# Feed-forward of a two-block kernel in four parts of 3, 3, 3 and 2 pieces instead of three of 4, 4 and 3, with a seventh pair of tiles for split weights

## The chip, the cores and the metric

The kernel runs on one core of one Trainium2 chip. The metric is the device time of one execution in microseconds. The kernel before took 1610.94 us (median of three runs, 1607.69 to 1611.66). The program is written in Python; a scheduler turns it into one fixed instruction list per engine, and the engines then run their lists in order and wait for each other through semaphores. Engines are named as in the profile: PE (TensorE matmul), PEld (its weight load), DVE (VectorE), ACT (ScalarE), POOL (GpSimd), SP (the queue that issues the weight loads).

## The reference, cut to what matters

Two transformer-like blocks run one after the other on 256 tokens of width 2048, all in float32. The change lies in the feed-forward of the first block:

```python
D_MODEL, SEQ, D_FF = 2048, 256, 5632
h2 = _rmsnorm(x, ffn_norm_w[l])
g, u = jnp.split(jnp.einsum('bsd,df->bsf', h2, w_gate_up[l]), 2, axis=-1)
x = x + jnp.einsum('bsf,fd->bsd', jax.nn.silu(g) * u, w_down[l])
```

Ahead of it stand the first block's mixer and its output projection, behind it a norm and the whole second block (input projection, short convolution, two kinds of attention, output projection), which the change does not touch.

## The kernel before, in words

**Split operands.** Every large product is made three times with operands cut into a high and a low part. A weight tile `raw` of 256 rows by 512 columns (512 KB) is loaded by SP; ACT writes its high part `wh` (L63), DVE the low part `wl` = raw - wh (L54), and PE multiplies high by high, high by low, and low by high. `parts_of` (L120) does the two splits and takes the pair of tiles (`wh`, `wl`) from a pool. In the feed-forward the list `more_w` (L642) says which pool is next: it is turned round by one at each split and holds `wsp` (four pairs) and `wsx` (two pairs), six pairs in all. A pair comes free when the last matmul that reads it is done, so PE sets when ACT and DVE may split the next weights; DVE in turn, by finishing a split, sets when a raw tile (eight of them) comes free for SP's next load.

**Units.** The left operands, already split, lie in units: tiles of 128 x 4 x 2 x 256 from `upool`, which has eight. During the feed-forward four units hold the normed input (`x1u`), and the others take the hidden activations.

**Pieces and parts.** The 5632 hidden columns are cut into eleven pieces of 512. `hidden_pre(f, between)` (L651) makes one piece: eight steps over 256 input rows each. Five steps split a gate and an up tile and make 24 matmuls; three steps (2, 4 and 6) use a seven-product form with sums of weights (`Ta`, `Tb`) and split tiles of 1024, 1024, 1024 and 512 columns for 21 matmuls. A piece thus has 183 matmuls of 512 columns, 22 splits, and at its end a chain of ten additions on DVE, two silu on ACT and two products (`hd`, L51) on DVE. It uses all eight PSUM banks.

**The turn.** The piece's result `hd` has tokens on partitions and must be turned round: `turn` (L735) makes eight 128 x 128 transposes on PE in two groups of four, and after each group ACT and DVE read the bank and write half a unit. The second group goes into the same bank as the first, so it waits for the first group to be read. Inside a part the turn of one piece is made in the middle of the next one, after its step 5 (`between(X4)`, L684), in the bank of that piece's accumulator X4, whose last six matmuls (step 8) then go into it again, once the second group has been read. The last piece of a part is turned by itself after it (`waiting(bank(...))`, L757).

**Down projection.** At the end of a part, `proj` (L149) multiplies the part's units with `w_down`, four times over, for 512 output columns each: 24 matmuls and two weight tiles for each unit and column group. `residual` (L593) then adds the two PSUM banks to `X` on DVE. In the last part each column group is also normed by its weight, transposed and split into `x2u`, for the second block.

**What sets the order.** The scheduler places ready instructions by priority; loads, splits and the end of a piece are raised by 4000 places. It may mix the matmuls of down projection and of the next or last piece on PE, as long as their operands come in order.

Of the kernel before, what the change touches and what calls it, by code (L numbers as in the profile page):

```python
# [9 lines left out]
F32R = mybir.dt.float32r  # L10
# [19 lines left out]
def tile_two_blocks(  # L30
# [12 lines left out]
    wsp = ctx.enter_context(tc.tile_pool(name="wsp", bufs=4))  # L43
    upool = ctx.enter_context(tc.tile_pool(name="upool", bufs=8))
# [8 lines left out]
    def tt(out, a, b, op):  # L53
        nc.vector.tensor_tensor(out=out, in0=a, in1=b, op=op)  # L54
# [7 lines left out]
    def act(out, in_, func=AF.Copy, **kw):  # L62
        nc.scalar.activation(out=out, in_=in_, func=func, **kw)  # L63
# [4 lines left out]
    def bank(shape):  # L68
        return phd.tile(shape, F32, tag="h", name="h")
# [5 lines left out]
    def new_unit():  # L75
        return upool.tile([128, 4, 2, T], F32R, tag="u", name="u")
# [10 lines left out]
    def unit_from(src, scale, u=None, js=range(2), keep=None):  # L87
        u = u or new_unit()
        for j in js:
            ps = transposed(src, j)  # L90
            if keep is not None:
                keep(j, ps)
            for a in range(2):
                k = 2 * j + a
                act(u[:, k, 0], ps[:, a], scale=scale(k))
                stt(u[:, k, 1], ps[:, a], scale(k), u[:, k, 0].bitcast(F32), ALU.mult, ALU.subtract)
        return u
# [8 lines left out]
    more_w = []  # L106
# [13 lines left out]
    def parts_of(raw, pool=None):  # L120
        if pool is None:
            pool = more_w[0] if more_w else wsp
            if more_w:
                more_w.append(more_w.pop(0))
        wh = pool.tile(list(raw.shape), F32R, tag="wh", name="wh")
        wl = pool.tile(list(raw.shape), F32R, tag="wl", name="wl")
        act(wh, raw)
        tt(wl, raw, wh.bitcast(F32), ALU.subtract)
        return wh, wl

    def split(w, r0, nk, c0, n, pool=None):
        with tc.high_priority(4000):
            return parts_of(load(w, r0, nk, c0, n), pool)
# [15 lines left out]
    def proj(units, w, c0, first_nk=2, after=None):  # L149

        pt = [mm_bank() for t in range(NT)]
        last = len(units) - 1
        for i, (u, r0) in enumerate(units):
            grow = u if callable(u) else None
            nk = first_nk if i == 0 else 2
            for k0 in range(0, 4, nk):
                if grow is not None and k0 % 2 == 0:
                    u = grow(k0 // 2)
                wh, wl = split(w, r0 + k0 * 128, nk, c0, CW)
                for a in range(nk):  # L160
                    k = k0 + a
                    mh, ml = in_turn(wh[:, a]), in_turn(wl[:, a])
                    for t in range(NT):
                        sl = slice(t * 128, (t + 1) * 128)
                        st, sp = i == 0 and k == 0, i == last and k == 3
                        nc.tensor.matmul(pt[t], lhsT=u[:, k, 0, sl], rhs=mh, start=st, stop=False)  # L166
                        nc.tensor.matmul(pt[t], lhsT=u[:, k, 0, sl], rhs=ml, start=False, stop=False)  # L167
                        nc.tensor.matmul(pt[t], lhsT=u[:, k, 1, sl], rhs=mh, start=False, stop=sp)  # L168
            if after is not None:
                after(i)  # L170
        return pt
# [37 lines left out]
    def stats_piece(st, src, c):  # L209
        for t in range(NT):  # L210
            nc.vector.bn_stats(out=st[:, t, c], in_=src(t))
# [341 lines left out]
    for hf in range(2):  # L553
# [5 lines left out]
        for j in range(2):  # L559
# [4 lines left out]
            for a in range(2):  # L564
                k = 2 * j + a
# [7 lines left out]
        u = new_unit()  # L573
# [8 lines left out]
    def xc(c):  # L582
        return lambda t: X[:, t, c * CW:(c + 1) * CW]

    def xk(c):
        return lambda t, k: X[:, t, c * CW + k * 128:c * CW + (k + 1) * 128]
# [6 lines left out]
    def residual(pt, c):  # L593
        for t in range(NT):
            x_c = two(xc(c)(t))
            tt(x_c, ordered(pt[t]), x_c, ALU.add)
# [42 lines left out]

    more_raw.extend([wraw, ff.enter_context(tc.tile_pool(name="wraw2", bufs=4))])  # L640
    wsx = ff.enter_context(tc.tile_pool(name="wsx", bufs=2))
    more_w.extend([wsp, wsp, wsx, wsp, wsp, wsx])  # L642

    def tri(pt, left, right, st, sp):
        (xh, xl), (wh, wl) = left, right
# [5 lines left out]
    def hidden_pre(f, between):  # L651
# [14 lines left out]
        for p in range(8):  # L666
# [21 lines left out]
            with tc.high_priority(4000):  # L688
                g_ = load(w_gate_up, r0, 2, f * CW, CW)
                u_ = load(w_gate_up, r0, 2, DFF + f * CW, CW)  # L690
                B1 = parts_of(g_)
                Ta, Tb = (fp.tile([128, 2, CW], F32, tag=n, name=n) for n in ("Ta", "Tb"))
                tt(Ta[:, 0], u_[:, 0], g_[:, 0], ALU.subtract)
                tt(Ta[:, 1], u_[:, 1], u_[:, 0], ALU.subtract)
                W13 = parts_of(Ta)
                tt(Tb[:, 0], u_[:, 1], Ta[:, 0], ALU.subtract)
                tt(Tb[:, 1], g_[:, 1], Tb[:, 0], ALU.subtract)
                W24 = parts_of(Tb)
                B22 = parts_of(u_[:, 1:2])
# [35 lines left out]
    def turn(h, u):  # L735
        def run(ps):
            ps = ps.rearrange("p (a t) -> p a t", a=2)
            for j in range(2):
                for a in range(2):
                    for t in range(NT):  # L740
                        nc.tensor.transpose(
                            out=ps[:, a, t * 128:(t + 1) * 128],
                            in_=h[:, t, 256 * a + j:256 * (a + 1):2], identity=ident,
                        )
                unit_split(u, ps, 2 * j, 2)
        return run

    st = new_stats()
    x2u = []
    for part in (range(0, 4), range(4, 8), range(8, 11)):  # L750
        gu = []
        waiting = lambda ps: None
        for f in part:
            h = hidden_pre(f, waiting)
            gu.append((new_unit(), f * CW))
            waiting = turn(h, gu[-1][0])
        waiting(bank([128, CW]))  # L757
        for c in range(4):
            residual(proj(gu, w_down, c * CW), c)
            if part[-1] == 10:  # L760
                x2u.append(unit_from(xk(c), lambda k, c=c: wfg[:, 4 * c + k:4 * c + k + 1]))
                stats_piece(st, xc(c), c)
# [291 lines left out]
    for u, r0 in out_units:  # L1054
        for k0 in (0, 2):
            pool = lw if len(parts) < 6 else wsp
            parts.append((u, k0, split(w_out2, r0 + k0 * 128, 2, 3 * CW, CW, pool)))
    for t in range(NT):
        sl = slice(t * 128, (t + 1) * 128)
        n = CW if t == 0 else CW // 2  # L1060
        for c0 in range(0, CW, n):
            pt = mm_bank()[:, :n]
            cs = slice(c0, c0 + n)
            for i, (u, k0, (wh, wl)) in enumerate(parts):
                for a in range(2):
                    k = k0 + a
# [7 lines left out]
            part = small.tile([128, 1], F32, tag="part", name="part")  # L1074
# [50 lines left out]
```

## Time and profile before

| | before |
|---|---|
| median of three runs | 1610.94 us |
| the profiled execution's own time | 1610.98 us |
| its span, first to last instruction | 1609.2 us |
| PE, DVE, ACT busy, share of the span | 99%, 77%, 55% |
| granted TensorE clock, mean | 0.999 |
| the feed-forward in the trace | about 530 to 1205 us |

The profiled execution took 1.8 us more than its span. In the views a row has a start and a duration in microseconds, the engine, the line, and the tiles as out<-in; in square brackets stands the idle time of the engine ahead of it and what ended it. Matmuls overlap: a 512-column matmul is shown with 0.38 us, but the next one starts 0.216 us after it.

### The profile page before, as it was taken

To read this page: it belongs to the slowest core of one execution; us is meant where nothing else is said; L and a number is where in the kernel's file an instruction comes from. 1 tells how busy PE (TensorE), PEld (TensorE's weight loads), DVE (VectorE), ACT (ScalarE), POOL (GpSimd) and SP (SyncE) were. 2 spreads that over 40 slices of the span, in tenths; PEclk is the share of its full clock that TensorE was granted. 3 is DMA by queue.
4 is the path that set the end of the run, shared out by engine and by line. 5 is a ranking of instruction groups with operands and counts; after the bars stand their busy time and mean duration, and the time that the engine had idled before them with its cause. 6 is when DMAs were issued, how large, how long until landed. Compare 5 with 4: busy or idle time off the path is not lost.

```text
span 1609.2 us, 22431 instructions
## 1 busy us (share of the span) xinstructions
PE 1591.8 (99%) x8433; PEld 1415.7 (88%) x8433; DVE 1241.6 (77%) x1726; ACT 886.0 (55%) x1156; POOL 23.0 (1%) x61
## 2 busy tenths in 40 slices
PE   9999999999999999999999999999999999999997
PEld 7999999999988888888888888888889889998987
DVE  7769768765667899976699975799777999766754
ACT  4657557544555665543565554456546545555644
POOL 2000000000000000000000000000000000000000
PEclk9999999999999999999999999999999999999999
DMA  8765466466686666676666676566756567556564
GB/s 283 225 192 166 145 178 188 143 186 209 203 301 216 183 199 207 203 236 202 191 208 199 188 241 205 181 210 198 242 151 207 146 199 222 182 157 199 163 218 140
DMA packets 164604, 318.36 MB, mean 198 GB/s; under 512 B 10184, under 2 KB 10848, under 8 KB 164496
## 3 DMA queue, kind: packets, MB, share of 16 engines
q1 hardware_dynamic: 162240, 312.25, 62.3%
q10 hardware_dynamic: 1760, 4.47, 0.8%
q8 instruction: 66, 1.08, 0.3%
q0 software_dynamic: 496, 0.21, 0.1%
q14 instruction: 42, 0.34, 0.1%
HBM read 313.74 MB, written 3.15 MB: 197 GB/s over the span
## 4 chain that ended last, share of the span: by engine, by line
PE 82%; DVE 12%; issue 3%; DMA 2%; ACT 0%; DVEq 0%; POOLq 0%; ACTq 0%; POOL 0%
PE p L194 18%; PE p L168 11%; PE p L167 11%; PE p L166 11%; PE p L195 9%; DVE wl L54 6%; PE p L648 3%; PE p L649 3%; PE p L647 3%; PE h L448 2%; PE h L649 2%; PE h L648 2%; PE h L647 2%; DMA raw<-in_w_gate_up_dram 2%; PE p L192 1%
## 5 line engine op out<-in xcount | busy, mean ns | idle before, releaser
L54 DVE TENSOR_TENSOR wl<-raw,wh 128x1024 fp32r<-128x1024 f32 (+1 forms) x580 | 682.3, 1186 | 272.8 <-ACT wh L63 270.4
L63 ACT ACTIVATE wh<-raw 128x1024 fp32r<-128x1024 f32 (+1 forms) x580 | 589.5, 1028 | 521.9 <-PE p L168 172.0
L194 PE MATMUL p<-u,wh 128*128 128x512 f32 x1392 | 458.6, 383 | 0.6 <-DVE sg L54 0.6
L195 PE MATMUL p<-u,wl 128*128 128x256 f32 x1392 | 365.7, 274 | 1.0 <-DVE wl L54 0.9
L167 PE MATMUL p<-wl,u 128*128 128x512 f32 x832 | 318.2, 383 | 0.0
L166 PE MATMUL p<-wh,u 128*128 128x512 f32 x832 | 313.6, 382 | 1.6 <-ACT u L63 1.1
L168 PE MATMUL p<-wh,u 128*128 128x512 f32 x832 | 313.6, 382 | 0.9 <-DVE u L51 0.9
L194 PEld LDWEIGHTS p<-u,wh 128*128 128x128 f32 x1392 | 260.1, 190 | 31.1 <-DVE sg L54 1.1
L195 PEld LDWEIGHTS p<-u,wl 128*128 128x128 f32 x1392 | 266.5, 191 | 8.4 <-DVE wl L54 1.7
L166 PEld LDWEIGHTS p<-wh,u 128*128 128x128 f32 x832 | 157.7, 190 | 24.2 <-ACT u L63 1.9
L168 PEld LDWEIGHTS p<-wh,u 128*128 128x128 f32 x832 | 157.3, 190 | 22.4 <-DVE u L51 1.3
L167 PEld LDWEIGHTS p<-wl,u 128*128 128x128 f32 x832 | 157.9, 190 | 21.6 <-DVE wl L54 0.2
L648 PE MATMUL p<-wl,u 128*128 128x512 f32 x341 | 129.9, 382 | 1.4 <-DVE wl L54 1.3
L649 PE MATMUL p<-wh,u 128*128 128x512 f32 x341 | 128.3, 379 | 0.0
L647 PE MATMUL p<-wh,u 128*128 128x512 f32 x341 | 123.7, 380 | 0.0
L648 PE MATMUL h<-wl,u 128*128 128x512 f32 x198 | 75.3, 380 | 1.4 <-DVE wl L54 1.4
L648 PEld LDWEIGHTS p<-wl,u 128*128 128x128 f32 x341 | 64.5, 189 | 12.8 <-DVE wl L54 3.9
L649 PE MATMUL h<-wh,u 128*128 128x512 f32 x198 | 75.1, 379 | 0.0
L647 PE MATMUL h<-wh,u 128*128 128x512 f32 x198 | 74.4, 381 | 0.3 <-DVE u L54 0.2
L647 PEld LDWEIGHTS p<-wh,u 128*128 128x128 f32 x341 | 64.5, 189 | 9.0
L649 PEld LDWEIGHTS p<-wh,u 128*128 128x128 f32 x341 | 64.5, 189 | 8.8
L54 DVE TENSOR_TENSOR Ta<-raw 128x512 f32<-128x512 f32 x66 | 42.5, 685 | 27.8 <-DMA raw<-in_w_gate_up_dram 27.6
(315 smaller groups left out, 1699.6 us busy)
## 6 DMA issues: line engine op xcount, KB each, us to landing
raw<-in_w_in_dram SPq DMA_DIRECT2D x232, 512.0 KB, 3.9
raw<-in_w_gate_up_dram SPq DMA_DIRECT2D x176, 512.0 KB, 4.5
raw<-in_w_down_dram SPq DMA_DIRECT2D x88, 512.0 KB, 4.9
raw<-in_w_out_dram SPq DMA_DIRECT2D x64, 512.0 KB, 4.9
raw<-in_w_mem_kv_dram SPq DMA_DIRECT2D x14, 512.0 KB, 5.7
xp<-in_x_dram SPq DMA_DIRECT2D x4, 512.0 KB, 6.0
X<-in_x_dram SPq DMA_DIRECT2D x4, 512.0 KB, 6.4
mp<-in_mem_dram SPq DMA_DIRECT2D x3, 512.0 KB, 8.2
```

The costliest lines, as they stand in the source:

```text
L54: nc.vector.tensor_tensor(out=out, in0=a, in1=b, op=op)
L63: nc.scalar.activation(out=out, in_=in_, func=func, **kw)
L166: nc.tensor.matmul(pt[t], lhsT=u[:, k, 0, sl], rhs=mh, start=st, stop=False)
L167: nc.tensor.matmul(pt[t], lhsT=u[:, k, 0, sl], rhs=ml, start=False, stop=False)
L168: nc.tensor.matmul(pt[t], lhsT=u[:, k, 1, sl], rhs=mh, start=False, stop=sp)
L192: nc.tensor.matmul(pt[f], lhsT=wh[:, a, fs], rhs=both, start=False, stop=True)
L194: nc.tensor.matmul(pt[f], lhsT=wh[:, a, fs], rhs=both, start=st, stop=False)
L195: nc.tensor.matmul(pt[f][:, :T], lhsT=wl[:, a, fs], rhs=high, start=False, stop=False)
L448: nc.tensor.matmul(ps[:, h], lhsT=k[:, h, s * 128:(s + 1) * 128], rhs=q[:, h, t * 128:(t + 1) * 128], start=True, stop=True,)
L647: nc.tensor.matmul(pt, lhsT=xh, rhs=mh, start=st, stop=False)
L648: nc.tensor.matmul(pt, lhsT=xh, rhs=ml, start=False, stop=False)
L649: nc.tensor.matmul(pt, lhsT=xl, rhs=mh, start=False, stop=sp)
```

## The change

`new_unit()` takes a unit from `upool`. With at most three pieces in a part, `x1u` and the hidden units hold seven of the eight units, and the eighth is entered in `more_w` as a seventh place: there a unit is cut into a `wh` and a `wl` half. The pieces are put into parts of 3, 3, 3 and 2.

```diff
@@ parts_of
-        wh = pool.tile(list(raw.shape), F32R, tag="wh", name="wh")
-        wl = pool.tile(list(raw.shape), F32R, tag="wl", name="wl")
+        if pool is upool:
+            u = new_unit()
+            wh, wl = (
+                u[:, i:i + 2].rearrange("p k a t -> p (k a t)")[:, :raw.shape[1] * raw.shape[2]]
+                .rearrange("p (k n) -> p k n", n=raw.shape[2]) for i in (0, 2)
+            )
+        else:
+            wh = pool.tile(list(raw.shape), F32R, tag="wh", name="wh")
+            wl = pool.tile(list(raw.shape), F32R, tag="wl", name="wl")
@@ feed-forward
-    more_w.extend([wsp, wsp, wsx, wsp, wsp, wsx])
+    more_w.extend([wsp, wsp, wsx, wsp, wsp, wsx, upool])
@@ feed-forward
-    for part in (range(0, 4), range(4, 8), range(8, 11)):
+    for part in (range(0, 3), range(3, 6), range(6, 9), range(9, 11)):
```

Behind the change lines stand seven numbers higher (the turn's transposes are L748, a piece's matmuls L654 to L656, the down projection's L173 to L175).

**The seventh pair on DVE, at the start of the feed-forward.** Before, the low parts of the weights there are all named `wl`:

```order
L54 TENSOR_TENSOR wl_5240<-Ta_5235,wh_5239 128x1024
L54 TENSOR_TENSOR wl_5212<-raw_5209,wh_5211 128x1024
L54 TENSOR_TENSOR F6_5030<-ss_5025,F6_5030 128x4x128
L54 TENSOR_TENSOR wl_5277<-raw_5274,wh_5276 128x1024
L54 TENSOR_TENSOR Ta_5320<-raw_5314,raw_5312 128x512
```

With the change, among the splits of the same steps, one goes into a unit (`u_5359`):

```order
L54 TENSOR_TENSOR wl_5245<-Tb_5235,wh_5244 128x1024
L54 TENSOR_TENSOR wl_5231<-raw_5226,wh_5230 128x1024
L54 TENSOR_TENSOR u_5359<-raw_5357,u_5359 128x1024
L54 TENSOR_TENSOR wl_5239<-Ta_5234,wh_5238 128x1024
L54 TENSOR_TENSOR wl_5275<-raw_5272,wh_5274 128x1024
```

A weight tile with a higher number (5357) than those behind it is split ahead of them, since a unit is free while the six old pairs are taken.

**The end of the last part on PE.** Before: the turn of the last piece (`hd_10204`), the piece's last six matmuls (into `h_9865`), and matmuls of the down projection (`p_...`) with the unit `u_9857` of the piece ahead:

```order
L741 MATMUL h_10220<-ident_81,hd_10204 128x128
L168 MATMUL p_10367<-wh_10388,u_9495 128x512
L166 MATMUL p_10366<-wh_10388,u_9495 128x512
L647 MATMUL h_9865<-wh_10185,u_5016 128x512
L648 MATMUL h_9865<-wl_10186,u_5016 128x512
L649 MATMUL h_9865<-wh_10185,u_5016 128x512
L647 MATMUL h_9865<-wh_10185,u_5016 128x512
L648 MATMUL h_9865<-wl_10186,u_5016 128x512
L649 MATMUL h_9865<-wh_10185,u_5016 128x512
L168 MATMUL p_10233<-wh_10291,u_9857 128x512
L168 MATMUL p_10234<-wh_10291,u_9857 128x512
L166 MATMUL p_10233<-wh_10291,u_9857 128x512
```

Now, at the same place: the second half of the turn of piece 9 (`hd_9962`), the last six matmuls of piece 10 into the same bank `h_9985`, then all eight transposes of piece 10 (`hd_10321`), and only then the down projection:

```order
L656 MATMUL h_9983<-wh_10302,u_5016 128x512
L748 MATMUL h_9985<-ident_81,hd_9962 128x128 x4
L654 MATMUL h_9985<-wh_10302,u_5016 128x512
L655 MATMUL h_9985<-wl_10303,u_5016 128x512
L656 MATMUL h_9985<-wh_10302,u_5016 128x512
L654 MATMUL h_9985<-wh_10302,u_5016 128x512
L655 MATMUL h_9985<-wl_10303,u_5016 128x512
L656 MATMUL h_9985<-wh_10302,u_5016 128x512
L748 MATMUL h_10337<-ident_81,hd_10321 128x128 x8
L173 MATMUL p_10350<-u_10354,u_9977 128x512
L173 MATMUL p_10351<-u_10354,u_9977 128x512
L173 MATMUL p_10446<-wh_10450,u_9977 128x512
```

Before, down matmuls of two finished units lie around the last piece's end; now none lies between its last gate-up matmuls, the turns and the transposes.

**The same end on DVE.** Before, the last half of the turn of piece 9 (`u_9857`), the sums and products of piece 10, and splits for the down projection:

```order
L54 TENSOR_TENSOR wl_10310<-raw_10307,wh_10309 128x1024
L54 TENSOR_TENSOR wl_10371<-raw_10368,wh_10370 128x1024
L54 TENSOR_TENSOR u2_10201<-h_9863,u2_10201 128x512
L54 TENSOR_TENSOR wl_10389<-raw_10386,wh_10388 128x1024
L51 SCALAR_TENSOR_TENSOR hd_10204<-u2_10201,rs1_5051,g_10203 128x512
L54 TENSOR_TENSOR u_9857<-h_9865,u_9857 128x2x256
L54 TENSOR_TENSOR wl_10328<-raw_10325,wh_10327 128x1024
L54 TENSOR_TENSOR wl_10425<-raw_10422,wh_10424 128x1024
L54 TENSOR_TENSOR x4_10104<-h_9865,x4_10104 128x512
L51 SCALAR_TENSOR_TENSOR hd_10204<-x4_10104,rs1_5051,g_10203 128x512
```

With the change, from the first `w_down` split (`wl_10372`) on: sums of the piece (`u2`, `u3`, `x4`, `g`), splits, the first half of piece 9's turn (`u_9977`):

```order
L54 TENSOR_TENSOR wl_10372<-raw_10369,wh_10371 128x1024
L54 TENSOR_TENSOR u2_10318<-p_9980,g_10320 128x512
L54 TENSOR_TENSOR wl_10390<-raw_10387,wh_10389 128x1024
L54 TENSOR_TENSOR u3_10319<-p_9981,u2_10318 128x512
L54 TENSOR_TENSOR wl_10408<-raw_10405,wh_10407 128x1024
L54 TENSOR_TENSOR wl_10451<-raw_10448,wh_10450 128x1024
L54 TENSOR_TENSOR x4_10221<-x4_10221,u3_10319 128x512
L54 TENSOR_TENSOR u_9977<-h_9985,u_9977 128x2x256
L54 TENSOR_TENSOR g_10320<-p_9979,g_10320 128x512
L54 TENSOR_TENSOR g_10320<-h_9984,u3_10319 128x512
```

and right behind these:

```order
L54 TENSOR_TENSOR wl_10469<-raw_10466,wh_10468 128x1024
L54 TENSOR_TENSOR x4_10221<-p_9982,x4_10221 128x512
L54 TENSOR_TENSOR u2_10318<-p_9982,u2_10318 128x512
L54 TENSOR_TENSOR u_9977<-h_9985,u_9977 128x2x256
L54 TENSOR_TENSOR u2_10318<-h_9983,u2_10318 128x512
L51 SCALAR_TENSOR_TENSOR hd_10321<-u2_10318,rs1_5051,g_10320 128x512
L54 TENSOR_TENSOR x4_10221<-h_9985,x4_10221 128x512
L51 SCALAR_TENSOR_TENSOR hd_10321<-x4_10221,rs1_5051,g_10320 128x512
L54 TENSOR_TENSOR wl_10487<-raw_10484,wh_10486 128x1024
L54 TENSOR_TENSOR u_10336<-h_10337,u_10336 128x2x256
```

Five splits for the down projection stand among the last piece's sums and turn; the second half of piece 9's turn (`u_9977` the second time) is the fourteenth in the list, the last product `hd_10321` the eighteenth.

Over the whole program PE, ACT and SP have as many instructions as before (8193 matmuls on PE in the list, 1130 on ACT, 606 on SP), and DVE has eight more, the additions to `X` of the fourth part.

## The prediction

> **What bounds the kernel now.** I read the page first, then busy times by stage, then waits, then single instructions.
>
> ```profile
> PE 1591.8 (99%) x8433; PEld 1415.7 (88%) x8433; DVE 1241.6 (77%) x1726; ACT 886.0 (55%) x1156; POOL 23.0 (1%) x61
> PE 82%; DVE 12%; issue 3%; DMA 2%; ACT 0%; DVEq 0%; POOLq 0%; ACTq 0%; POOL 0%
> ```
>
> PE is busy 99% of the span and carries 82% of the chain that ended last; DVE carries 12%. So time can be won only where PE waits, and is lost wherever PE is made to wait. In the feed-forward, cut at the places where its parts and pieces change (columns: stretch, its length, then busy time and count for PE, PEld, DVE, ACT, POOL, then clock and DMA):
>
> ```profile
> 541.00:600.00 59.00, 59.00 (x276) 51.72 (x276) 49.95 (x60) 38.58 (x43) 0.00 (x0) 1.00 0.67 207
> 600.00:670.00 70.00, 68.33 (x317) 58.23 (x316) 66.45 (x82) 37.49 (x45) 0.00 (x0) 1.00 0.62 194
> 670.00:772.00 102.00, 102.00 (x482) 89.60 (x481) 70.64 (x74) 49.40 (x52) 0.00 (x0) 1.00 0.70 220
> 772.00:850.00 78.00, 78.00 (x365) 68.38 (x364) 65.92 (x78) 46.07 (x51) 0.00 (x0) 1.00 0.60 187
> 850.00:910.00 60.00, 58.61 (x274) 49.93 (x273) 56.38 (x71) 32.88 (x39) 0.00 (x0) 1.00 0.63 201
> 910.00:1019.00 109.00, 109.00 (x513) 95.74 (x514) 77.34 (x82) 52.96 (x56) 0.00 (x0) 1.00 0.71 218
> 1019.00:1093.00 74.00, 74.00 (x345) 64.80 (x344) 63.42 (x75) 43.08 (x48) 0.00 (x0) 1.00 0.63 198
> 1093.00:1138.00 45.00, 45.00 (x216) 39.59 (x215) 43.67 (x53) 27.61 (x32) 0.00 (x0) 1.00 0.65 205
> ```
>
> Where PE never pauses, PEld is busy 0.877 of the time (51.72 of 59, 68.38 of 78, 64.80 of 74). In 600 to 670 it has 58.23, which at 0.877 is 66.4 us of work in 70: 3.6 us lost. In 850 to 910 it has 49.93, 56.9 us of work in 60: 3.1 us lost. Everywhere else nothing is lost, the ends of parts (670 to 772, 910 to 1019) and the whole third part (1019 to 1138) included. Both losses lie late in a part of four pieces, and DVE is busy 95% there (66.45 of 70) and 94% (56.38 of 60).
>
> PE's own busy column shows only 1.7 and 1.4 us of pause at these places, 3.1 in all. [...]
>
> ```profile
> 643.22 0.38 PE L649 MATMUL h<-wh,u 128*128 128x512 f32 x1
> 643.43 0.38 PE L647 MATMUL h<-wh,u 128*128 128x512 f32 x1
> 644.62 0.48 PE L648 MATMUL h<-wl,u 128*128 128x512 f32 x1 [0.81 <-DVE wl L54]
> DVE wl L54 <- ACT wh L63: 71.5, 66, 1.9
> DVE Ta L54 <- DMA raw<-in_w_gate_up_dram: 26.1, 10, 3.6
> ```
>
> A matmul follows the last one after 0.21 us, but here after 1.19: 0.98 us are lost where only 0.81 are shown as idle. PE waited for a low part from DVE; DVE itself had waited (last two rows, 541 to 1138 us: total, times, longest) for ACT, which waits for a free pair, and for raw tiles from memory.
>
> **The change, part by part.** *Parts of three.* The third part shows what a part of three pieces does that starts as the second does (no loss in 772 to 850 nor in 1019 to 1093): it loses nothing. So the 3.1 us of the second part go, whatever the seventh pair does. In the first part the piece that moves out is the fourth, of which this row holds the loss:
>
> ```profile
> 660.00:670.00 10.00, 9.74 (x46) 8.21 (x45) 10.00 (x13) 4.84 (x6) 0.00 (x0) 1.00 0.63 195
> ```
>
> 8.21 instead of 8.77: 0.6 us. *The seventh pair* lets ACT and DVE be one split further ahead. A piece has 22 splits and 183 x 0.216 = 39.5 us of matmuls, so one split is 1.8 us of PE time. It adds lead, not speed: with DVE at 95% a lead once spent is hardly filled again, so of the 3.0 us left in the first part it saves 1.8 at most and nothing at least; I take the middle, 0.9. No instruction is added for it. Together 3.1 + 0.6 + 0.9 = 4.6 us won, bounds 0 and 6.7.
>
> *The fourth part's additions.* Eight more `X` additions on DVE, and in the last part, with two units in place of three, less PE time to hide a column group's work:
>
> ```profile
> L54 DVE TENSOR_TENSOR X<-p,X 128x512 f32<-128x512 f32 x22 | 14.3, 685 | 2.4 <-PE p L168 2.4
> L51 DVE SCALAR_TENSOR_TENSOR u<-h,wfg,u 128x256 fp32r<-128x256 f32 x12 | 5.4, 475 | 1.7 <-ACT u L63 1.7
> L211 DVE BATCH_NORM_STATS2 bst<-X 128x6 f32<-128x512 f32 x6 | 3.8, 680 | 0.0
> ```
>
> The additions are 8 x 0.685 = 5.5 us in stretches where DVE idles 31 of 102 us. A column group of the last part has 48 x 0.216 = 10.4 us on PE; DVE has at most 4 splits of 1.22, 2 x 0.685, 4 x 0.475 and 2 x 0.680, together 9.5. Both are hidden, at 0; without that cover the second would cost 4 groups x the excess, of which there is none. Loads stay the same in number and size, SP's list keeps its length, and a load still waits for a raw tile.
>
> *The end of the last part.* Here the new order leaves PE without other work, and the sum of it is the main term. With two pieces, piece 9 is the only other unit, and its own turn is made inside piece 10. The prices are those of the same steps at the end of the third part before:
>
> ```profile
> 1131.74 3.90 ACT L63 ACTIVATE wh<-raw 128x1024 fp32r<-128x1024 f32 x4
> 1132.78 0.69 DVE L54 TENSOR_TENSOR u<-p,g 128x512 f32<-128x512 f32 x1 [0.16 <-PE p L649]
> 1133.39 1.21 DVE L54 TENSOR_TENSOR wl<-raw,wh 128x1024 fp32r<-128x1024 f32 x1
> 1134.52 0.68 DVE L54 TENSOR_TENSOR u<-p,u 128x512 f32<-128x512 f32 x1
> 1143.77 0.63 PE L741 MATMUL h<-ident,hd 128*128 128x128 f32 x4
> 1144.16 0.46 PE L168 MATMUL p<-wh,u 128*128 128x512 f32 x1
> 1144.56 0.58 ACT L63 ACTIVATE u<-h 128x512 fp32r<-128x512 f32 x1
> 1152.55 0.38 PE L649 MATMUL h<-wh,u 128*128 128x512 f32 x1
> 1152.97 0.69 DVE L54 TENSOR_TENSOR x<-h,x 128x512 f32<-128x512 f32 x1 [1.47 <-PE h L649]
> 1153.70 0.75 DVE L51 SCALAR_TENSOR_TENSOR hd<-x,rs,g 128x512 f32<-128x512 f32 x1
> ```
>
> From one start to the next a split takes DVE 1.13 us (1133.39 to 1134.52), a short sum 0.61, a high part 0.98 on ACT (3.90 for four); four transposes hold PE 0.39 (1143.77 to 1144.16); ACT starts to read them 0.79 after their start and takes 0.58, DVE then about 0.69; the `x4` sum starts 0.42 after X4's last matmul, `hd` 0.73 after that and ends 0.75 later. I set the clock to 0 where PE frees the pair that the first down split, `wl_10372`, takes: by rotation that of the split seven places earlier, the first of step 7 (`wl_10240`, six matmuls). PE then still has 6 + 6 + 3 matmuls of that step, 24 of step 8 and eight transposes: 39 x 0.216 + 0.78 = 9.2 us to the transposes of `hd_10321`. ACT and DVE need: the high part to 1.1; up to the first half of piece 9's turn 4 splits and 4 short ones, to 8.1; from there to the second half one split and 5 short ones, to 12.2. Only then may PE start X4's last six matmuls, since they go into that bank; they and the 0.42 end at 13.7, `x4` and `hd` at 15.2. PE stands 6.0 us. The second group of `hd_10321`'s transposes shares the bank with the first and comes 0.79 + 0.58 + 0.69 after its start, PE's own 0.39 of that aside: 1.7 more. Then 20 matmuls with piece 9's unit follow, which the splits behind can meet. Together 7.7 us lost. Before, the same steps cost PE nothing, since down matmuls filled them. What is queued behind the waiting transposes on PE is the whole down projection of the last part, so all of the loss reaches the end.
>
> The bounds: if DVE were never late, the three dependent steps alone still cost 1.7 for piece 9's second half, 1.7 for X4's sums (0.42 + 0.73 + 0.75 less one 0.216) and 1.7 for the second group, 5.0 in all, which is the low end; a further wait of 1.9 (the longest of DVE for ACT, above) makes 9.6. I take 7.7, because the list gives DVE 18 instructions there and their prices have rows.
>
> *The sum:* 1609.2 - 4.6 + 7.7 = 1612.3 us of span. The profiled execution took 1610.98, 1.8 more than its span, and the median of the runs is 1610.94; so 1614.1 us, 0.2% over the median.
>
> **The rivals.** 0.3% of the median, about what a measurement of this kernel can tell from no change, is 4.8 us: faster is below 1606.1, slower above 1615.8.
>
> *The clock falls in the pause (slower).* The longest stand without a break is between the second group of piece 9's turn (8.1 to about 8.6, for it waits for the first half) and 12.2: 3.6 us. The trace shows a fall after such a time, at its end, and what a low clock costs, at its start:
>
> ```profile
> 1600.89 0.28 PE L1071 MATMUL p<-wh,u 128*128 128x256 f32 x1
> 1600.00:1605.00 5.00, 1.17 (x11) 0.97 (x9) 1.73 (x4) 1.84 (x4) 0.54 (x1) 0.98 0.13 48
> 1605.00:1609.20 4.20, 0.00 (x0) 0.00 (x0) 0.00 (x0) 0.00 (x0) 0.00 (x0) 0.50 0.56 193
> 9.51 0.79 PE L166 MATMUL p<-wh,u 128*128 128x512 f32 x1 [0.88 <-ACT u L63]
> 10.52 0.63 PE L166 MATMUL p<-wh,u 128*128 128x512 f32 x1
> 10.95 0.63 PE L167 MATMUL p<-wl,u 128*128 128x512 f32 x1
> 14.28 0.38 PE L167 MATMUL p<-wl,u 128*128 128x512 f32 x1
> ```
>
> The last matmul ends at 1601.2; a mean of 0.98 over five microseconds is 0.2 at half clock, so the clock fell at about 1604.8, 3.6 us later. At the start matmuls come 0.43 apart, from 9.51 to 14.28: 4.8 us at half clock, 2.4 lost, and the two shorter pauses would draw it out to about 3. That is 1617, and it decides from a stand of about 3.6 us on. Against it: that is the very length. Chance 0.12. [...]
>
> *Splits out of turn (slower).* DVE's list now has unit splits ahead of splits that PE wants first. Each puts those behind off by 1.13 us; in the stretch without slack, three unit splits a piece, one piece of waits would cost 3.4 us: 1617.5. For it speaks DVE's 95%; against it that in 1093 to 1138 DVE is busy 97% (43.67 of 45) and PE loses nothing. Chance 0.12.
>
> *Small pause, full gain (no change).* 5.0 lost and 6.7 won: 1609.3. Chance 0.17.
>
> *The pause is covered and the gain is had (faster).* 1611.0 - 4.6 to 6.7, 1604 to 1606. PE's list would have to run something between, and it has nothing there. Chance 0.06. That the pair is not used is excluded by the order.
>
> **How the numbers follow.** The forecast has 0.53, with 1612 to 1616.5 of its own: 0.40 of it below 1615.8, 0.13 above. No change: 0.40 + 0.17 = 0.57. Slower: 0.13 + 0.12 + 0.12 = 0.37. Faster: 0.06. The range takes the small pause at its foot and the slower rivals at its head: 1608.5 to 1618.
>
> **What would show it.** In the trace of the changed kernel the transposes of the last turn (L748) should stand apart from the matmuls ahead of them, PE idle in three pieces (before X4's last six, about 3.6 us; before the first four transposes, about 2; before the second four, about 1.7), with DVE as releaser. PEld should be at 0.877 through the second and third part and below it only in the first. The DVE sums should run without a gap from the first down split on. The prediction is wrong if PE has no pause at the last turn, if the first part's loss vanishes or doubles, or if the clock shows less than 1.0 behind the turn.

## The result, and the profile after

The changed kernel takes 1623.87 us (median of five runs, 1622.37 to 1624.56), the kernel before 1610.05 (five runs, 1607.69 to 1611.66): a ratio of 1.0086, 95% interval 1.0075 to 1.0097. It is 13.8 us slower; the forecast was 1614.1, with a range up to 1618.0.

Two rows of the page of the changed kernel (busy time by engine; the chain that ended last) and its span with the mean granted clock:

```profile
PE 1596.0 (98%) x8433; PEld 1418.1 (87%) x8433; DVE 1247.8 (77%) x1734; ACT 886.7 (55%) x1156; POOL 24.3 (1%) x61
PE 87%; DVE 7%; DMA 3%; issue 2%; ACT 1%; POOL 0%; SPq 0%; POOLq 0%; DVEq 0%; ACTq 0%
core 0: 1622.6 us, clock 0.994
```

The work is the same, and PE is still nearly always busy; the page hardly tells the two kernels apart. Both traces have 8433 matmul records, so the n-th matmul of one can be set against the n-th of the other. How much later the changed kernel starts it:

| n-th matmul | starts before at | later by | what lies ahead |
|---|---|---|---|
| 3000 | 527 | +0.5 us | already there at matmul 150, at 37 us, before anything differs |
| 3150 | 559 | +2.5 | **start of the feed-forward: 2.0 lost** |
| 5850 | 1140 | +1.7 | the parts: 0.8 won |
| 6000 | 1171 | +12.5 | **end of the last part: 10.9 lost** |
| 6450 | 1251 | +13.0 | last down projection: 0.5 lost |
| 8432 | 1601 | +13.4 | near the end of the program: 0.4 lost |

The records count transposes too, which take PE 0.1 us each (0.39 for four) where a 512-column matmul takes 0.216. At the 5850th record the kernel before has made four transposes more, so half a microsecond belongs one row further down: with that put right the parts win 1.3 and the end of the last part loses 11.3.

By stretches (length, then busy time and count for PE, PEld, DVE, ACT, POOL, then clock and DMA), the changed kernel:

```profile
600.00:676.00 76.00, 73.68 (x348) 63.37 (x348) 64.15 (x76) 40.60 (x48) 0.00 (x0) 1.00 0.65 212
676.00:1010.00 334.00, 334.00 (x1564) 293.03 (x1563) 277.34 (x317) 179.94 (x197) 0.00 (x0) 1.00 0.63 204
1010.00:1060.00 50.00, 49.29 (x237) 43.11 (x236) 37.04 (x41) 25.30 (x28) 0.00 (x0) 1.00 0.69 222
1150.00:1180.00 30.00, 23.16 (x96) 18.83 (x95) 20.14 (x24) 12.92 (x16) 0.00 (x0) 0.83 0.49 162
```

and the kernel before, in the stretches where its first and second part lose time:

```profile
600.00:676.00 76.00, 74.33 (x345) 63.48 (x344) 72.45 (x89) 41.55 (x50) 0.00 (x0) 1.00 0.62 193
676.00:1010.00 334.00, 332.61 (x1559) 290.53 (x1558) 259.85 (x291) 173.64 (x188) 0.00 (x0) 1.00 0.67 209
```

With the prediction's full share of 0.877, the changed kernel loses 3.7 us in 600 to 676 (63.37 is 72.3 us of work in 76), as much as before (63.48, 3.6 lost); nothing in 676 to 1010, where the kernel before loses 2.7 (290.53 is 331.3 of 334); 0.8 in 1010 to 1060; and in 1150 to 1180 PEld has 21.5 us of work in 30.

**The last turn**, on PE, in the changed kernel (start, duration, in brackets the idle time ahead and what ended it):

```profile
1160.94 0.74 PE L748 MATMUL h<-ident,hd 128*128 128x128 f32 x4 [0.62 <-DVE u L54]
1165.06 0.48 PE L654 MATMUL h<-wh,u 128*128 128x512 f32 x1 [3.38 <-DVE u L54]
1166.36 0.63 PE L655 MATMUL h<-wl,u 128*128 128x512 f32 x1
1166.79 0.63 PE L656 MATMUL h<-wh,u 128*128 128x512 f32 x1
1169.06 0.92 PE L748 MATMUL h<-ident,hd 128*128 128x128 f32 x3 [1.43 <-DVE hd L51]
1171.39 1.13 PE L748 MATMUL h<-ident,hd 128*128 128x128 f32 x4 [1.41 <-DVE u L54]
```

and the clock there, in short windows:

```profile
1165.50:1166.00 0.50, 0.50 (x4) 0.39 (x3) 0.47 (x2) 0.00 (x0) 0.00 (x0) 0.68 0.77 254
1166.00:1167.00 1.00, 1.00 (x4) 0.82 (x3) 0.39 (x1) 0.00 (x0) 0.00 (x0) 0.50 0.39 147
1175.00:1176.00 1.00, 1.00 (x4) 0.81 (x3) 0.00 (x0) 0.00 (x0) 0.00 (x0) 0.54 0.70 264
1176.00:1177.00 1.00, 1.00 (x6) 0.86 (x6) 0.00 (x0) 0.00 (x0) 0.00 (x0) 1.00 0.01 2
```

The forecast stands are there, one after the other (3.38, 1.43, 1.41, with 0.62 ahead). From 1159.94 to the first matmul behind 1176.0, 16.1 us pass for 16 matmuls and 12 transposes, which at full rate are 4.6: 11.5 us lost. Behind the long stand the clock is at half: a mean of 0.68 in the half microsecond to 1166.0 puts its fall at 1165.68, the 0.54 its return at 1175.92. Of these 10.24 us PE stood 2.84 (1.43 + 1.41), so 7.4 ran at half speed and cost 3.7. The waits are the other 7.8. That the fall is not of this one execution alone is likely from the mean granted clock: 0.992 to 0.995 in all five, 0.996 to 0.999 in the fast executions of the kernel before.

**The start of the feed-forward.** In the changed kernel a sum of weights (`Tb`) of the first piece goes into a unit:

```profile
530.40 1.06 ACT L63 ACTIVATE u<-Tb 128x1024 fp32r<-128x1024 f32 x1
532.03 1.22 DVE L54 TENSOR_TENSOR u<-Tb,u 128x1024 fp32r<-128x1024 f32 x1
533.30 0.48 PE L655 MATMUL p<-u,F 128*128 128x512 f32 x1 [0.24 <-DVE u L54]
535.18 0.48 PE L654 MATMUL p<-wh,u 128*128 128x512 f32 x1 [0.74 <-ACT wh L63]
536.52 0.45 PE L654 MATMUL h<-wh,u 128*128 128x512 f32 x1 [0.65 <-DVE u L51]
```

and in the kernel before the same split goes into an ordinary pair:

```profile
529.40 1.22 DVE L54 TENSOR_TENSOR wl<-Tb,wh 128x1024 fp32r<-128x1024 f32 x1
```

It comes 2.6 us later (532.03 against 529.40, 0.5 of it the start-up), and PE waits for it and for what is pushed behind it.

### The profile page after: what moved, and what is told of

It reads as the page before. It is cut to its first block, busy times and chain, and to the rows that moved or that the text cites. A ratio compares the mean times of both kernels' runs of the same rounds, so it can differ in the third digit from the quotient of the medians.

```text
span 1622.6 us, 22400 instructions
## 1 busy us (share of the span) xinstructions
PE 1596.0 (98%) x8433; PEld 1418.1 (87%) x8433; DVE 1247.8 (77%) x1734; ACT 886.7 (55%) x1156; POOL 24.3 (1%) x61
## 4 chain that ended last, share of the span: by engine, by line
PE 87%; DVE 7%; DMA 3%; issue 2%; ACT 1%; POOL 0%; SPq 0%; POOLq 0%; DVEq 0%; ACTq 0%
PE p L201 17%; PE p L175 10%; PE p L174 10%; PE p L173 10%; PE p L202 9%; PE p L655 5%; PE p L656 5%; PE p L654 5%; PE h L656 3%; PE h L655 3%; PE h L654 3%; DVE wl L54 3%; PE h L455 2%; PE p L199 1%; DMA raw<-in_w_out_dram 1%
## 5 line engine op out<-in xcount | busy, mean ns | idle before, releaser
L54 DVE TENSOR_TENSOR wl<-raw,wh 128x1024 fp32r<-128x1024 f32 (+1 forms) x542 | 639.5, 1190 | 250.7 <-ACT wh L63 248.4
L63 ACT ACTIVATE wh<-raw 128x1024 fp32r<-128x1024 f32 (+1 forms) x542 | 553.0, 1032 | 505.4 <-PE p L175 150.0
L174 PE MATMUL p<-wl,u 128*128 128x512 f32 x784 | 300.3, 384 | 1.0 <-DVE wl L54 0.9
L173 PE MATMUL p<-wh,u 128*128 128x512 f32 x784 | 296.1, 384 | 2.8 <-ACT u L63 1.6
L175 PE MATMUL p<-wh,u 128*128 128x512 f32 x784 | 295.7, 383 | 0.6 <-DVE u L51 0.6
L173 PEld LDWEIGHTS p<-wh,u 128*128 128x128 f32 x784 | 149.1, 191 | 24.7 <-ACT wh L63 2.3
L174 PEld LDWEIGHTS p<-wl,u 128*128 128x128 f32 x784 | 149.2, 190 | 22.3 <-DVE wl L54 2.0
L175 PEld LDWEIGHTS p<-wh,u 128*128 128x128 f32 x784 | 148.8, 190 | 21.2 <-DVE u L51 1.0
L655 PE MATMUL p<-wl,u 128*128 128x512 f32 x293 | 111.4, 380 | 0.2 <-DVE wl L54 0.2
L656 PE MATMUL p<-wh,u 128*128 128x512 f32 x293 | 110.7, 379 | 0.0
L654 PE MATMUL p<-wh,u 128*128 128x512 f32 x293 | 109.4, 380 | 0.7 <-ACT wh L63 0.7
L654 PE MATMUL h<-wh,u 128*128 128x512 f32 x168 | 63.6, 383 | 4.0 <-DVE u L54 3.4
L655 PE MATMUL h<-wl,u 128*128 128x512 f32 x168 | 64.3, 383 | 0.0
L656 PE MATMUL h<-wh,u 128*128 128x512 f32 x168 | 64.1, 382 | 0.0
L654 PEld LDWEIGHTS p<-wh,u 128*128 128x128 f32 x293 | 55.4, 189 | 8.9 <-ACT wh L63 1.1
L655 PEld LDWEIGHTS p<-wl,u 128*128 128x128 f32 x293 | 55.4, 189 | 8.4 <-DVE wl L54 0.6
L656 PEld LDWEIGHTS p<-wh,u 128*128 128x128 f32 x293 | 55.4, 189 | 7.7
L54 DVE TENSOR_TENSOR Ta<-raw 128x512 f32<-128x512 f32 x66 | 42.8, 684 | 21.5 <-DMA raw<-in_w_gate_up_dram 21.5
```

Of the source, the lines that this page charges most:

```text
L654: nc.tensor.matmul(pt, lhsT=xh, rhs=mh, start=st, stop=False)
L655: nc.tensor.matmul(pt, lhsT=xh, rhs=ml, start=False, stop=False)
L656: nc.tensor.matmul(pt, lhsT=xl, rhs=mh, start=False, stop=sp)
```

## The experiments

Ratios are against the kernel before, run on the same chip in turn, with 95% intervals. The profiled executions differ by up to 2.2 us by the 150th matmul, where all these kernels still do the same, and not again until the feed-forward. So spans alone don't decide; stalls and medians do. A stretch of one trace is good to about 1 us: the changed kernel, turn_early and skip are alike up to the last part, and lose 3.7, 4.6 and 4.8 in 600 to 676.

| | parts | seventh pair | us | ratio |
|---|---|---|---|---|
| changed kernel | 3, 3, 3, 2 | from the shared pool | 1623.9 | 1.0086 (1.0075 to 1.0097) |
| p3332_six | 3, 3, 3, 2 | none | 1607.7 | 0.9980 (0.9971 to 0.9990) |
| p2333_seven | 2, 3, 3, 3 | from the shared pool | 1646.2 | 1.0226 (1.0200 to 1.0251) |
| p2333_six | 2, 3, 3, 3 | none | 1608.3 | 0.9993 (0.9983 to 1.0003) |
| turn_early | 3, 3, 3, 2 | from the shared pool | 1620.0 | 1.0065 (1.0048 to 1.0083) |
| skip | 3, 3, 3, 2 | shared, not for one split | 1616.8 | 1.0042 (1.0027 to 1.0057) |
| own7 | 3, 3, 3, 2 | one unit, held | 1608.6 | 0.9991 (0.9981 to 1.0000) |
| own7_late | 3, 3, 3, 2 | held, from piece 1 on | 1606.7 | 0.9980 (0.9970 to 0.9989) |
| own7_2333_late | 2, 3, 3, 3 | held, from piece 1 on | 1606.1 | 0.9976 (0.9966 to 0.9985) |

### The parts alone

```diff
-    more_w.extend([wsp, wsp, wsx, wsp, wsp, wsx, upool])
+    more_w.extend([wsp, wsp, wsx, wsp, wsp, wsx])
```

> Parts 3, 3, 3, 2 as in the change, but without the seventh pair. What is to be split: against the kernel before, the changed one lost 2.0 us at the start of the feed-forward, won only 0.8 in its parts and lost 10.9 at the end of the last part. Theory: the losses at the start and in the parts come from the pair (unit splits set ahead of others), the loss at the end from the parts. Then here: start 0.4 lost as before, first part 2.8 (3.4 less the 0.6 of its fourth piece), second and third part nothing, end of the last part 11 to 12 with the clock at 0.5 behind it; in all 1610 - 3.5 + 11.5 = 1618 us. Rival: the parts themselves change the order of the splits, and the pair is nothing or a help: start 2.0 and first part 4 lost as in the changed kernel or more, 1624 us or above.

Measured: 1607.7, ten below the expectation of my own theory. Same stretches as above, this kernel:

```profile
600.00:676.00 76.00, 75.58 (x357) 65.50 (x357) 66.72 (x78) 40.83 (x47) 0.00 (x0) 1.00 0.67 215
676.00:1010.00 334.00, 333.69 (x1563) 292.32 (x1562) 278.57 (x320) 181.93 (x198) 0.00 (x0) 1.00 0.66 204
1010.00:1060.00 50.00, 50.00 (x239) 44.01 (x238) 35.49 (x38) 22.86 (x26) 0.00 (x0) 1.00 0.71 223
1150.00:1180.00 30.00, 30.00 (x147) 26.27 (x146) 24.74 (x30) 15.57 (x19) 0.00 (x0) 1.00 0.59 191
```

The end of the last part loses nothing, with the same two pieces in it. So it was not the part of two pieces that left PE without cover. PE now has down matmuls (L173 to L175) around the turns, here around the second half of piece 9's turn (first three rows) and within the last turn:

```profile
1155.74 0.38 PE L173 MATMUL p<-wh,u 128*128 128x512 f32 x1
1156.82 0.63 PE L748 MATMUL h<-ident,hd 128*128 128x128 f32 x4
1157.20 0.68 PE L175 MATMUL p<-wh,u 128*128 128x512 f32 x2
1167.97 0.38 PE L173 MATMUL p<-wh,u 128*128 128x512 f32 x1
1168.19 0.51 PE L748 MATMUL h<-ident,hd 128*128 128x128 f32 x3
```

The parts win about what was forecast of them, 3.7: 1.3 us are lost in 600 to 676 (65.50 is 74.7 of 76) in place of 3.6, and 0.7 in 676 to 1010 (292.32 is 333.3) in place of 2.7, which makes 4.3 won. By the n-th matmul it is 3.3 from the 3150th to the 5850th.

### The part of two pieces first

```diff
-    for part in (range(0, 3), range(3, 6), range(6, 9), range(9, 11)):
+    for part in (range(0, 2), range(2, 5), range(5, 8), range(8, 11)):
```

> The seventh pair stays, the part of two pieces stands first (2, 3, 3, 3). Theory: the whole loss at the end comes from two pieces being too few to cover the last turn; with three at the end, as before, the turn costs nothing and the clock stays at 1.0: 11.5 us less than the changed kernel, 1612 us; less than that, down to 1609, if the first part with its early down projection no longer uses up the lead. Rival: the seventh pair (a unit held for splits at the last turn) makes the loss at the end; then it stays, 1620 us or above.

> Parts 2, 3, 3, 3 without the seventh pair: neither suspect. Theory: no loss at the end, 0.4 at the start, the second to fourth part lose nothing (three pieces each), the first at most 1: against 6.7 lost in the feed-forward before this is 1604 to 1606 us. Rival: what is used up is the lead from the start of the feed-forward on, whatever the parts; then some 3.4 stay to be lost between 600 and 670, and 1607 to 1608 comes out. With the kernel that keeps the pair beside it: if the pair costs 2.0 at the start and as much in the parts, this one is 2 to 5 us faster than that.

Measured: 1646.2 with the pair, 1608.3 without. My theory, that three pieces at the end mend it, fell as far as it could: with the pair this order is the slowest of all. The long stands are now at several turns, here at the end of the last part, on PE and, below, on DVE:

```profile
1152.05 0.63 PE L748 MATMUL h<-ident,hd 128*128 128x128 f32 x4
1156.45 1.13 PE L748 MATMUL h<-ident,hd 128*128 128x128 f32 x4 [3.77 <-DVE u L54]
```

```profile
1153.44 2.36 DVE L54 TENSOR_TENSOR wl<-raw,wh 128x1024 fp32r<-128x1024 f32 x2 [2.92 <-ACT wh L63]
1155.71 0.69 DVE L54 TENSOR_TENSOR u<-h,u 128x512 fp32r<-128x512 f32 x1
1156.31 1.22 DVE L54 TENSOR_TENSOR u<-raw,u 128x1024 fp32r<-128x1024 f32 x1
```

The two kernels differ in the pair alone, and by 38 us. Without it, the parts' order matters little (1608.3 against 1607.7). The kernel without it should have come to 1604 to 1606 and did not: its trace has few stalls left in the feed-forward (0.7 us in 600 to 676, 0.6 in 676 to 1010, by PEld) and starts the last matmul 4.1 us sooner than before, 0.9 of it start-up, but its median is only 2.3 lower, and its interval takes in 1. The rival's time (1607 to 1608) came out without its cause, the 3.4 us between 600 and 670. That leaves the pair. How it does this is not shown here; the last row, a split into a unit (`u<-raw,u`) right behind a write into a hidden unit (`u<-h,u`), says where to look.

### More work behind the wait

```diff
-                prod(b, x_(a, t), (wh[:, a], wl[:, a]), a == 1 and (end or (b is X4 and p == 5)))
-                if p == 5:
+                prod(b, x_(a, t), (wh[:, a], wl[:, a]), a == 1 and (end or (b is X4 and p == (3 if f == 10 else 5))))
+                if p == (3 if f == 10 else 5):
```

> The changed kernel, but in piece 10 alone the turn of piece 9 is made after step 4 instead of step 6 of the eight, so that twelve matmuls of X4 and most of the two last steps lie behind the wait for its second half. Theory: the stand of 3.4 us ahead of X4's last matmuls goes and with it the clock's fall; X4's sum (1.7) and the second group of the last turn (1.7) stay, so 3.5 to 4 of the 11.5 us are left: 1616 us, clock 1.00 behind the turn. If the clock alone (about 4 of the 11.5) were to go and the waits stayed: 1620. Rival: DVE is so late there that the stand only moves to the next wait; 1622 to 1624, clock at 0.5 again.

The code counts a piece's steps from 0, the expectation from 1: the turn moves from behind `p == 5` to behind `p == 3`.

Measured: 1620.0, the figure expected if only the clock were mended, but that is not what happened. The stand ahead of X4's last six matmuls is gone, and another stands in its place, ahead of the last turn's transposes:

```profile
1164.37 0.39 PE L748 MATMUL h<-ident,hd 128*128 128x128 f32 x1 [2.30 <-DVE hd L51]
1166.17 0.63 PE L748 MATMUL h<-ident,hd 128*128 128x128 f32 x3 [1.41 <-DVE hd L51]
1168.21 1.13 PE L748 MATMUL h<-ident,hd 128*128 128x128 f32 x4 [1.42 <-DVE u L54]
```

The rival (the stand moves to the next wait, the clock falls) is right in what happens, though its 1622 to 1624 was not reached. As long as no down matmul can stand between, the chain of sums, product and transposes is waited for somewhere. The clock still falls (0.50 from 1168 to 1173), though no stand is longer than 2.30.

### Which split goes into the unit

The order of ACT's list shows the place. In the changed kernel, around the last turn (`hd` of piece 10 goes into `u_10336`):

```
785 L63 ACTIVATE wh_10450<-raw_10448 128x1024
786 L63 ACTIVATE u_9977<-h_9985 128x2x256
787 L63 ACTIVATE wh_10468<-raw_10466 128x1024
788 L63 ACTIVATE g_10320<-g_10320,rs1_5051 128x512
789 L63 ACTIVATE u_9977<-h_9985 128x2x256
790 L63 ACTIVATE g_10320<-g_10320,rs1_5051 128x512
791 L63 ACTIVATE wh_10486<-raw_10484 128x1024
792 L63 ACTIVATE u_10336<-h_10337 128x2x256
793 L63 ACTIVATE u_10354<-raw_10352 128x1024
```

`raw_10352` is the first tile of the last down projection; its turn of pools gave it a unit, and its split (`u_10354`) stands behind six others with higher numbers, and behind the first half of the last turn. PE's list begins the down projection with it, so no down matmul can run ahead of the turn. The list does not say why the split is set there; in the program the unit asked for just ahead of it, from the same pool, is the last turn's own, `u_10336`. The next two experiments take that split, and then all of them, out of the sharing. The first:

```diff
         waiting(bank([128, CW]))
+        if part[-1] == 10 and more_w[0] is upool: more_w.append(more_w.pop(0))
         for c in range(4):
```

> The changed kernel, but where the turn of pools would give the first down split of the last part a unit, it is passed over: that split takes an ordinary pair, and the units go on with the next turn. Without the seventh pair the same four parts lost nothing at the end, so two pieces are cover enough; the new theory is that the first tile of the last down projection, split into a unit, is set behind the last turn in ACT's and DVE's lists, and with it every down matmul that could cover the turn. Then the loss at the end goes whole, 11 us, and the rest stays (2.0 at the start, 4 in the first part, 1 at 1050): 1613 us, clock 1.00 behind the turn. Rival: what makes DVE late there is the number of unit splits around the turn, not this one; 6 us or more of the 11 stay, 1618 or above.

Measured: 1616.8, 7.1 below the changed kernel. By the n-th matmul the end of the last part costs 0.3 us (10.9 in the changed kernel), with the clock at 1.00: that one split held the cover back:

```profile
1150.00:1180.00 30.00, 29.20 (x142) 25.46 (x141) 21.37 (x25) 15.56 (x19) 0.00 (x0) 1.00 0.65 202
```

The expectation of 1613 missed by 3.8: some 1 us is lost right behind the last turn, at 1175, and 2.4 in the second block's input projection, at 1235:

```profile
1229.89 1.42 DVE L51 SCALAR_TENSOR_TENSOR X<-X,rsf,rw 128x512 f32<-128x512 f32 x2 [1.26 <-DMA rw<-in_final_norm_w_dram]
1234.95 0.38 PE L202 MATMUL p<-u,wl 128*128 128x256 f32 x1 [1.48 <-DVE wl L54]
```

DVE had waited for a norm weight from memory shortly before; whether that is the whole of it was not tried.

```diff
         if pool is upool:
-            u = new_unit()
+            u = held[0]
@@ feed-forward
     more_w.extend([wsp, wsp, wsx, wsp, wsp, wsx, upool])
+    held.append(new_unit())
```

> The changed kernel, but the seventh pair is one unit, taken once ahead of the feed-forward and held for splits to its end; the hidden activations have the three others. So a split never waits for, or stands ahead of, a hidden unit. Theory: at the end nothing is lost (11 us less); the stalls in the down projection of the first part (1.2 at 668) and of the third (1.0 at 1050) go too; the 2.0 at the start stay, since there no unit is free until the mixer's are, whoever holds it: 1624 - 11 - 2 = 1611 us. Rival: the order in which pairs come free, not the sharing with hidden units, makes the stalls inside the parts; then only the end is mended, 1613 or above.

Measured: 1608.6, 15.3 below the changed kernel with the same number of splits into units, in the same turn. The end loses nothing, and neither does the first part:

```profile
600.00:676.00 76.00, 76.00 (x363) 66.75 (x362) 67.82 (x79) 41.40 (x48) 0.00 (x0) 1.00 0.69 223
1010.00:1060.00 50.00, 49.29 (x235) 43.05 (x234) 33.76 (x37) 22.73 (x24) 0.00 (x0) 1.00 0.68 216
1150.00:1180.00 30.00, 30.00 (x148) 26.59 (x147) 23.95 (x29) 14.64 (x18) 0.00 (x0) 1.00 0.57 176
```

So the stalls at the end and in the first part come from splits and hidden units sharing one pool. Two things differ from the expectation: the start loses 1.3 us and not 2.0, and the stall in the third part's down projection stays (43.05 is 49.1 of 50, as in the changed kernel). So sharing is not the cause of that stall, nor of most of the loss at the start. Nor is a seventh pair as such the cause of the stall: the next kernel has one there and loses 0.2.

### A pair of its own, from the second piece on

```diff
-    more_w.extend([wsp, wsp, wsx, wsp, wsp, wsx, upool])
+    more_w.extend([wsp, wsp, wsx, wsp, wsp, wsx])
+    held.append(new_unit())
@@ feed-forward, both kernels; the second with parts 2, 3, 3, 3
             h = hidden_pre(f, waiting)
+            if f == 0:
+                more_w.append(upool)
```

> As the kernel with the held unit, but the seventh pair comes into use only behind the first piece. Theory: the start loses 0.5 as without the pair, so 1.5 us less than the kernel with the held unit from the start. Whether a seventh pair is worth anything by itself shows against the four parts without it (1607.7, with 2.4 us of stalls left in the feed-forward): if lead helps, those go to under 1 and 1606 comes out; if it does not, 1607.5 to 1609.

> Parts 2, 3, 3, 3 with the held unit from the second piece on. The same parts with the shared units took 1646, without a seventh pair 1608.3. Theory: all 36 us of stalls came from splits and hidden units sharing one pool; then they go here, 1606 to 1609 us, and no stall at a last turn is longer than 1 us. Rival: seven pairs upset DVE's order as such; then 10 us or more of them stay, above 1618.

Measured: 1606.7, between its two cases and nearer to the one in which lead helps, and 1606.1, as expected; the stalls of the parts 2, 3, 3, 3 with the shared pair are gone (from 541 to 1215 no pause of PE costs more than 0.5 us). For these parts two things changed at once, whose unit it is and from when it is used; for 3, 3, 3, 2 the held unit from the start tells them apart. In the first of the two:

```profile
600.00:676.00 76.00, 76.00 (x363) 66.91 (x362) 66.94 (x78) 41.10 (x47) 0.00 (x0) 1.00 0.68 222
1010.00:1060.00 50.00, 49.79 (x237) 43.66 (x236) 33.23 (x38) 21.77 (x24) 0.00 (x0) 1.00 0.70 222
```

The start costs 0.2 us more than before, as with six pairs, and the third part's down projection loses 0.2 (43.66 is 49.8 of 50) where the held unit used from the start lost 0.9. With the later entry the seventh place also falls on other splits; which of them makes those two losses was not tried. 66.91 is all of the 76 us: in this trace the 1.3 us of the first part's loss that the parts alone leave are gone, the gain of the seventh pair, though hardly more than two traces of like work can differ by. The two are 0.2% faster than the kernel before; from each other and from the parts alone (0.9980) the intervals don't tell them apart.

## Why the prediction was wrong

The forecast was 4.6 us won and 7.7 lost, 3.1 together; the spans differ by 13.4. The missing 10.3 are 5.8 in the gain, 3.2 at the end of the last part, 0.8 behind it, and 0.5 of start-up (rounded; without the four transposes 5.3 and 3.6).

- **Parts of three: 3.1 + 0.6 won.** Right in the sum, as the parts alone show: 4.3 by weight loads, 3.3 by the n-th matmul. The shares were off. The first part wins 2.3 (3.6 to 1.3), where one row of the fourth piece had given 0.6; the stretch of the second part wins 2.0 (2.7 to 0.7) and not all of its loss.
- **The seventh pair: "saves 1.8 at most and nothing at least".** This step failed. The bound below excluded a loss because no instruction is added. But a split that has the turn to a unit can only take a unit, not another pair, and units are also what hidden activations, and at the start the mixer's results, live in. With the pair the start loses 2.0 (0.2 with six pairs), the first part 2.4 more (3.7 against 1.3), the third part's down projection 0.8 and the end of the last part nearly all of its 11.3; the same parts without it take 1607.7 us and not 1623.9. Holding one unit for splits takes away the loss at the end, that of the first part and 0.7 of the start; the rest goes when the pair comes in a piece later, for a reason left open. The gain of 0.9 shows as 1.3 us of one trace where the pair shares with nobody; the medians (1606.7 against 1607.7) do not show it.
- **Splits out of turn (rival, 0.12, 3.4 us).** The right suspicion with the wrong sign. I had seen a split with a higher number ahead of others and priced the ones behind it. What costs is the reverse, a unit split set far behind its neighbours, and the matmuls that cannot run until it is made.
- **The end of the last part: 7.7.** The size of the waits was right: 7.8 us, in the places forecast (I had 3.6, 2 and 1.7; the stands shown as idle were 3.38, 1.43 and 1.41, with 0.62 ahead). That is not luck, since the sum priced the order as it stood. The cause was wrong. I read "no down matmul lies between" from the order, and put it down to two pieces; the same parts without the pair have them there. The order names the cause in one row (`u_10354`, the first down tile, behind `u_10336`), which I had read only as the first operand of PE's list.
- **The clock (rival, 0.12, 3 us, from a stand of 3.6 on).** It fell, and cost 3.7, which the sum had put at nothing; a clock below 1.0 behind the turn was one of the signs named for being wrong. The length of 3.6 was wrong: here the clock fell to 0.50 behind a shown stand of 3.38, and with the earlier turn to 0.50 where no shown stand was longer than 2.30.
- **The additions of `X`** are hidden, as forecast: with six pairs and four parts, the third part's down projection has PEld busy 44.01 of the 50 us from 1010 to 1060, which is all of them.

## What to carry to other kernels

A buffer that "comes free" is only spare if the work that may take it can also go elsewhere when it is taken: in a fixed rotation, a split that must have that buffer is put off, and so is all work that needs it first. When a new order lacks cover, follow the first operand that the missing work needs back to its place on the other engines before blaming the shape of the work, and try the two halves of a change apart: here one half won 0.2% and the other lost 1%.

## What the runs showed of the hardware

**The clock was at half for 10.24, 6.84 and 3.42 us, and PE had not stood still all the way to any of the three falls.** The three stretches are those of the changed kernel (1165.68 to 1175.92), of the kernel with the earlier turn (1167.04 to 1173.88) and one of the kernel with parts 2, 3, 3, 3 and the shared pair (917.40 to 920.82). The bounds come from windows like these, of the kernel with the earlier turn:

```profile
1164.00:1165.00 1.00, 0.39 (x1) 0.20 (x1) 1.00 (x2) 0.00 (x0) 0.00 (x0) 1.00 0.95 291
1165.00:1166.00 1.00, 0.00 (x0) 0.00 (x0) 1.00 (x2) 0.00 (x0) 0.00 (x0) 1.00 0.40 143
1166.00:1167.00 1.00, 0.63 (x3) 0.44 (x3) 0.11 (x1) 0.17 (x1) 0.00 (x0) 1.00 0.31 72
1167.00:1168.00 1.00, 0.00 (x0) 0.00 (x0) 0.54 (x1) 1.00 (x2) 0.00 (x0) 0.52 0.97 297
1173.00:1174.00 1.00, 1.00 (x4) 0.81 (x3) 0.00 (x0) 0.00 (x0) 0.00 (x0) 0.56 0.00 0
```

and of the kernel with parts 2, 3, 3, 3 and the shared pair:

```profile
915.00:916.00 1.00, 0.19 (x1) 0.19 (x2) 1.00 (x3) 0.87 (x1) 0.00 (x0) 1.00 0.88 270
916.00:917.00 1.00, 0.61 (x5) 0.42 (x5) 1.00 (x2) 0.41 (x1) 0.00 (x0) 1.00 1.02 395
917.00:918.00 1.00, 1.00 (x4) 0.79 (x5) 1.00 (x2) 0.40 (x2) 0.00 (x0) 0.70 0.99 346
920.00:921.00 1.00, 1.00 (x4) 0.78 (x4) 0.96 (x2) 0.00 (x0) 0.00 (x0) 0.59 1.06 356
```

With the earlier turn PE was busy 1.02 of the 3.04 us from 1164.00 to the fall (0.39 + 0.63), in the kernel with parts 2, 3, 3, 3 about 1.2 of the 2.40 from 915.00 (0.19 + 0.61 and the 0.4 to the fall), and in the changed kernel 0.62 of the 3.68 from 1162.00 (it starts again at 1165.06), by the modelled ends of matmuls. The longest shown stands ahead of these falls are 2.30, 2.62 and 3.38 us. So the length of one stand, by which the prediction went (3.6), did not tell these falls. What brings a fall is not shown.
